# Expert weights in 16 KB runs, and the modulation's bias pieces in turns of their own

## The chip, the core and the metric

One Trainium2 chip; the kernel runs on one of its cores, in one launch. The metric is the device time in microseconds. Shorter is better.

## What is computed

Two transformer blocks one after the other, in float32. There are 256 tokens of width 1024 (16 learned ones go before them in the first block). The first block has two kinds of attention side by side, a gated join, and a SwiGLU layer. The second modulates its input with a vector made from `c`, runs retention and dilated attention, joins them, and ends in a mixture of 32 experts of which each token takes 4:

```python
def second_block(x, c, w_ada, ...):
    cs = jax.nn.silu(c)
    mod = cs @ w_ada[l] + b_ada[l]                  # 6 x 1024 values
    sh_a, sc_a, gt_a, sh_f, sc_f, gt_f = jnp.split(mod, 6, axis=-1)
    h = modulate(rms_norm(x, g_mix[l]), sh_a, sc_a)
    ret, att = retention(...), dilated_attention(...)
    merged = sigmoid(ga) * (ret @ w_ret_o) + sigmoid(gb) * (att @ w_att_o)
    x = x + gt_a * (merged @ w_o)
    h = modulate(rms_norm(x, g_ffn[l]), sh_f, sc_f)
    x = x + gt_f * moe(h, ...)
    return rms_norm(x, g_final)

def expert_block(xb, e):                            # in moe, for each of 32 experts
    u = xb @ w1[e] + b1[e]                          # 1024 x 2048, 8 MB
    glu, lin = clipped u[:, ::2], clipped u[:, 1::2]
    return (glu * sigmoid(1.702 * glu) * (lin + 1)) @ w2[e] + b2[e]   # 1024 x 1024, 4 MB
```

## The kernel before, in words

The program is written out as straight code in two stages.

**Dense stage.** All matrix products but the experts' are "w" and "t_" operations in a list, `plan`. Each takes a weight tile of 1 MB (128 partitions x 2048 values) that `feed_loads` (line 137) loads through the SyncE (SP) queue into a ring of two. `feed_halves` (155) splits a half of a tile into a high and a low part: ScalarE copies the high part (line 106) and VectorE subtracts (107). Three halves of split operands (`SPL`) can stand ready. TensorE multiplies them in three products (lines 213 to 215) in `run_w`: 12 matmuls for each of two column groups of a half, and after each 12 a call of `tick` (176). `tick` moves the side work on: attention heads, norms, and `ada`, each a generator that yields the number of ticks that it wants to rest. So the place of side work in the engines' order is set by ticks, when the program is built. When heads are closed (`close_heads`, 558), ticks run without matmuls between them.

**Modulation and biases.** `ada` (251) makes the 48 columns of `mod`: a row of 128 x 1024 values is loaded by `row` (265) through the GpSimd (POOL) queue, and one VectorE instruction (line 280) multiplies it by `cs` and sums it. From row 18 on (`LAG["bp"]`), each turn begins with a piece of `bias_parts` (987): a load of expert biases (994), six GpSimd instructions that split them into three bfloat16 parts (995 to 1000), and a store (1001). There are six pieces. Rows and pieces share one pool tag, `wa`, with two buffers. While `st["hold"]` is set (around the last down products of the first block), `ada` rests. The order of a turn is

```python
            if j >= LAG["bp"]:
                next(more, 0)
            if j < 47:
                rows.append(row(j + 1))
            yield LAG["ada"]
```

**Expert stage.** 384 weight tiles of 1 MB come in a fixed sequence: for each expert 8 of w_mlp1 (line 1055, 128 runs of 8 KB), then 4 of the expert before of w_mlp2 (1057, 256 runs of 4 KB); the last four (1064) in runs of 2 KB. Tiles of 8 KB per partition, "homes", take them in turn, 21 of them (`where`, line 1040): some are freed buffers of the dense stage (tags `b` and `c`), some are pools opened when parts of the dense stage close. `mload` (1043) issues loads through SP up to a number of tiles, `mst["room"]`, that grows from 5 to 13 while the dense stage runs; from then on a load is written behind each tile that TensorE has used, 21 tiles ahead. The first product is at line 1265 (8 matmuls per tile), the second at 1299. Per expert there are also transposes (1283), a weighted sum (1316) and, every second expert, a gather of tokens (1189). `last_tile` (1352) handles the last expert's second product.

**Buffers.** `big` has a tag `b` of 10 buffers with 8 KB per partition; a `pair` (high and low part) takes two.

Of the kernel before, what the change touches and what calls it, by code (L numbers as in the profile page):

```python
# [20 lines left out]
P = 128  # L21
D = 1024
S = 256
# [13 lines left out]

LAG = dict(rs=2, ad0=1, lam=4, bq=12, el=4, bp=18, r1=52, wo=3, rg=21, ada=7, head=6, ffn=2, n2=3, n2b=6, sb0=4, sb1=6, vt=3, df0=1, df1=4, df2=3, df3=8, df4=4, rt0=6, rt1=6, dl0=2, dl1=4, dl2=11, dl3=1)
LAG["in"] = 4
# [3 lines left out]
def tile_two_blocks(ctx, tc, A, out, dbg=None):  # L43
# [26 lines left out]
    def bigt(name, n=S, dt=F32, k=KT, wide=False):  # L70
        if n > S or wide:
            return big.tile([P, k, n], dt, tag="c", name=name, bufs=3)
        return big.tile([P, k, n], dt, tag="b", name=name, bufs=10)

    def pair(name, n=S, wide=False):
        return bigt(name + "h", n, F32R, wide=wide), bigt(name + "l", n, F32R, wide=wide)

    def flat(name):
        return big.tile([P, 2048], F32, tag="b", name=name, bufs=10)

# [10 lines left out]
    nr = flat("nr")  # L91
    sqa, sqb, sqg, rs0, rr = nr[:, 0:512], nr[:, 512:1024], nr[:, 1024:1536], nr[:, 1536:1792], nr[:, 1792:2048]
    ones, tri, ident = (cst.tile([P, P], F32, tag="c_" + n, name=n) for n in ("ones", "tri", "ident"))
# [157 lines left out]
    def ada():  # L251
# [30 lines left out]


# [44 lines left out]
    def norm_in():  # L328
        h, l = pair("xn", L)
        st["xn"] = (h, l)  # L330
        a = tmp.tile([P, 2, L], F32, tag="wa", name="sqa", bufs=2)
        b = flat("sqt")[:, 0:6 * L].rearrange("p (k i n) -> p k i n", k=3, i=2)
        for k in range(0, KT, 2):
# [180 lines left out]
    def branch(name, mov, key, nk=8):  # L514

        def first(c):
            def f(ps):
                if c == 0:
                    st[key] = bigt(key)
# [144 lines left out]
    def norm2(sq):  # L664
# [13 lines left out]
        st["r2"] = r2.unsqueeze(1).to_broadcast([P, 2, S])  # L678
        f = bigt("f2")
        for k in (0, 4):  # L680
# [42 lines left out]
    for c in range(4):  # L723
        def rgs(ps, c=c):
            if c == 0:
                st["rg"] = bigt("rg")
            while "r2" not in st:
                tick()
            if c == 0:
                st["shw"] = tmp.tile([P, KT], F32, tag="shw", name="shw", bufs=1)  # L730
# [67 lines left out]
    def dil_pair(jp):  # L798
# [18 lines left out]
        def bias():  # L817
            if jp == 0:
                at = bigt("at", S, F32R)
                st["at"] = at[:, 0:4, :], at[:, 4:8, :]  # L820
# [63 lines left out]
    def open_ret():  # L884
        nonlocal hd
        close_heads(dil_head)
        pools["mra"] = ctx.enter_context(tc.tile_pool(name="mra", bufs=3, side="right", reuse_waits="tile"))
        hd = heads.enter_context(tc.tile_pool(name="hd3", bufs=2, side="right", reuse_waits="tile"))
        mst["room"] = 8
        st["dec"] = hd.tile([P, 4, S], F32, tag="dec", name="dec", bufs=1)  # L890
# [3 lines left out]
    def close_ret():  # L894
        close_heads(ret_head)
        pools["mrb"] = ctx.enter_context(tc.tile_pool(name="mrb", bufs=2, side="right", reuse_waits="tile"))
        mst["room"] = 10

# [11 lines left out]


    branch("w_att_o_2", lambda: st["at"], "yat", 4)
    for c in range(4):
# [58 lines left out]
    def moe_consts():  # L972
        q = nc.scalar
        m = cst.tile([P, 1024], F32, tag="m", name="m")
        st["gtf"], st["iota"], st["spare"] = m[:, 0:512], m[:, 768:992], m[:, 992:1024]
# [11 lines left out]
    def bias_parts():  # L987

        nc.gpsimd.dma_start(sel, A["sel"])
        for c in range(6):  # L990
# [10 lines left out]
            nc.gpsimd.dma_start(bsd.ap()[:, c_], r)  # L1001
            yield

# [35 lines left out]
    pools, own = {}, {}  # L1039
    where = ["b"] * 5 + ["mra"] * 3 + ["mrb"] * 2 + ["b"] * 3 + ["mrc"] * 2 + ["mrd"] * 3 + ["c"] + ["mre"] * 2 + ["c"]  # L1040
    R = len(where)

    def mload(upto):
        while mst["load"] <= min(upto, mst["room"] - 1):
            i = mst["load"]
            kind, e, k = seq[i]
            j = i % R
            if where[j] in "bc":
                if j not in own:
                    own[j] = big.tile([P, 2048], F32, tag=where[j], name="mw", bufs=10 if where[j] == "b" else 3)  # L1050
                t = own[j]
            else:
                t = pools[where[j]].tile([P, 2048], F32, tag="mw", name="mw")
            if kind == 1:
                nc.sync.dma_start(t, A["w_mlp1_2"][e, k * P:(k + 1) * P, :])
            elif e < NE - 1:
                nc.sync.dma_start(t.rearrange("p (k n) -> p k n", k=2),
                                  A["w_mlp2_2"][e, k * 2 * P:(k + 1) * 2 * P, :].rearrange("(k p) n -> p k n", p=P))
            else:

                src = A["w_mlp2_2"][e, k % 2 * 512:(k % 2 + 1) * 512, k // 2 * 512:(k // 2 + 1) * 512]
                for kk in range(0, 4, 4 if k < 3 else 2):
                    n = 4 if k < 3 else 2
                    nc.sync.dma_start(t.rearrange("p (k n) -> p k n", k=4)[:, kk:kk + n], src.rearrange("(k p) n -> p k n", p=P)[:, kk:kk + n])
            wt[kind, e, k] = t
            mst["load"] += 1

# [12 lines left out]
    for o in plan:  # L1080
# [4 lines left out]
        if key == ("w_ffn_gate", LAG["el"]):  # L1085
            mst["room"] = 5
        if key == ("w_in_2", 12):
# [4 lines left out]
        if o is plan[-1]:  # L1092
            break
        mst["room"] = {("w_in_2", 33): 12, ("w_ret_o_2", 3): 13}.get(key, mst["room"])
        for _ in range(3 if state["load"] == len(wops) else 1):
            if mst["load"] < mst["room"]:
                mload(mst["load"])
    mload(mst["room"] - 1)
# [52 lines left out]
    mm(rpv[:, 1, :], tris, mask[:, 1, :], start=False, stop=True)  # L1151
    ht = flat("ht").rearrange("p (t d) -> p t d", t=2)
    xps += [residual(c) for c in range(2, 4)]
# [39 lines left out]

    xeb = flat("xe")
    xe = [xeb[:, b * 1024:(b + 1) * 1024].rearrange("p (k n) -> p k n", k=KT) for b in range(2)]
# [6 lines left out]

    pools["mrc"] = ctx.enter_context(tc.tile_pool(name="mrc", bufs=2, reuse_waits="tile"))
    pools["mrd"] = ctx.enter_context(tc.tile_pool(name="mrd", bufs=3, reuse_waits="tile"))
    mt = ctx.enter_context(tc.tile_pool(name="mt", bufs=2, reuse_waits="tile"))
    pools["mre"] = ctx.enter_context(tc.tile_pool(name="mre", bufs=2, reuse_waits="tile"))
    pu = ctx.enter_context(tc.tile_pool(name="pu", bufs=2, space=PSUM, reuse_waits="tile"))
# [223 lines left out]
    with tc.If(items > 0):  # L1431
        with tc.For_i(0, items, 1) as it:
# [20 lines left out]
            for k in range(KT):  # L1453
                z = lw[3 + k % 3]
                nc.sync.dma_start(z, A["w_mlp1_2"][bass.ds(ex, 1), k * P:(k + 1) * P, :].rearrange("o p n -> p (o n)"))
                up_k(u, xx[:, k, :], lambda hf, c: z[:, hf * 1024 + c * 512:hf * 1024 + (c + 1) * 512], k)
# [4 lines left out]
            for k2 in range(4):  # L1461
                z = lw[3 + (k2 + 2) % 3]
                nc.sync.dma_start(z.rearrange("p (k n) -> p k n", k=2),
                                  A["w_mlp2_2"][bass.ds(ex, 1), k2 * 2 * P:(k2 + 1) * 2 * P, :].rearrange("o (k p) n -> p (o k) n", p=P))
                for kk in range(2):
# [98 lines left out]
def layout(inp):  # L1564
# [39 lines left out]
```

## Time and profile before

| | us |
|---|---|
| median of three runs | 1827.83 |
| lowest and highest | 1824.49, 1828.0 |
| the profiled execution | 1826.24 |
| its span, first to last instruction | 1824.0 |
| TensorE, VectorE, ScalarE, GpSimd busy | 1739.4, 875.0, 484.7, 123.9 |

The span has 25,881 instructions; 571.82 MB are moved, 313 GB/s over the whole, in 107,645 packets. Mean granted TensorE clock 0.986. A matmul is counted busy from its start to its modelled end, and matmuls overlap, so a busy TensorE is not one at its peak; the number of matmuls in a stretch tells more. "Idle before" is the time in which an engine stood before an instruction, with what ended it. The lines named are those of the kernel before.

### The profile page before, as it was taken

How to read it: one execution, taken by the hardware profiler on the slowest of the kernel's cores; microseconds unless marked ns; L12 is line 12 of the kernel's file. 1: busy time of each engine (PE TensorE's matmuls, PEld its weight loads, DVE VectorE, ACT ScalarE, POOL GpSimd, SP SyncE). 2: the span in 40 equal slices, each digit the busy share in tenths (PEclk: the TensorE clock that was granted, in tenths of full speed). 3: DMA queues.
4: the chain of work that ended last, by engine and by line, in shares of the span. 5: the costliest groups of instructions: out<-in, count | busy, mean ns of one | idle time of the engine just before them, and what ended most of it. 6: DMA issues, size and time to landing. Idle time of an engine off the chain costs nothing. (4 is left out here: it accounts for less than half of the span.)

```text
span 1824.0 us, 25881 instructions
## 1 busy us (share of the span) xinstructions
PE 1739.4 (95%) x10942; PEld 1145.8 (63%) x10942; DVE 875.0 (48%) x1330; ACT 484.7 (27%) x754; POOL 123.9 (7%) x132
## 2 busy tenths in 40 slices
PE   8999998789999999999999999999999999999987
PEld 7999998789998999999733333333233323332322
DVE  7767776577778667776422223222222222222223
ACT  4545654244435644455300000000000000000001
POOL 2100004520003000000100000000000000000000
PEclk8999999799999999999999999999999999999999
DMA  6446455468665654566899999999999999999996
GB/s 220 170 167 229 158 193 186 167 209 341 245 216 179 245 179 168 204 223 226 309 416 424 423 425 424 424 422 424 422 425 424 423 424 423 424 423 425 422 425 261
DMA packets 107645, 571.82 MB, mean 313 GB/s; under 512 B 11022, under 2 KB 16070, under 8 KB 59654
## 3 DMA queue, kind: packets, MB, share of 16 engines
q1 hardware_dynamic: 96144, 538.46, 74.1%
q0 software_dynamic: 7904, 28.08, 4.6%
q10 hardware_dynamic: 3478, 3.59, 0.6%
q8 instruction: 87, 1.43, 0.3%
q14 instruction: 32, 0.26, 0.0%
HBM read 568.44 MB, written 4.02 MB: 314 GB/s over the span
## 5 line engine op out<-in xcount | busy, mean ns | idle before, releaser
L1265 PE MATMUL u<-mw,xe 128*64 128x512 f32 x2048 | 476.7, 600 | 18.1 <-DMA mw<-in_w_mlp_dram 17.3
L107 DVE TENSOR_TENSOR hl<-w,hl 128x1024 fp32r<-128x1024 f32 (+1 forms) x256 | 318.3, 1257 | 146.6 <-ACT hl L106 146.1
L1265 PEld LDWEIGHTS u<-mw,xe 128*64 128x64 f32 x2048 | 132.7, 136 | 300.1 <-issue 222.8
L106 ACT ACTIVATE hl<-w 128x1024 fp32r<-128x1024 f32 (+1 forms) x256 | 260.1, 1032 | 125.2 <-PE ps L215 74.7
L1299 PE MATMUL y<-mw,aT 128*64 128x512 f32 x992 | 227.7, 597 | 19.6 <-DMA mw<-in_w_mlp_dram 19.4
L1299 PEld LDWEIGHTS y<-mw,aT 128*64 128x64 f32 x992 | 67.2, 136 | 163.2 <-issue 102.0
L1319 DVE TENSOR_TENSOR macc<-macc,cp 128x512 f32<-128x512 f32 x124 | 79.7, 684 | 184.4 <-PE cp L1316 184.4
L213 PE MATMUL ps<-xnh,hl 128*128 128x256 f32 (+1 forms) x512 | 153.3, 299 | 2.4 <-ACT hl L106 2.4
L215 PE MATMUL ps<-xnh,hl 128*128 128x256 f32 (+1 forms) x512 | 149.2, 291 | 6.2 <-DVE hl L107 6.2
L214 PE MATMUL ps<-xnl,hl 128*128 128x256 f32 (+1 forms) x512 | 148.2, 289 | 0.0
L1285 ACT COPY aT<-ap 128x512 f32<-128x512 f32 x31 | 18.2, 586 | 425.6 <-PE ap L1283 425.6
L213 PE MATMUL ps<-h2h,hl 128*128 128x256 f32 x384 | 110.2, 287 | 0.0
L215 PE MATMUL ps<-h2h,hl 128*128 128x256 f32 x384 | 108.7, 283 | 0.0
L214 PE MATMUL ps<-h2l,hl 128*128 128x256 f32 x384 | 108.6, 283 | 0.0
L213 PEld LDWEIGHTS ps<-xnh,hl 128*128 128x128 f32 x512 | 99.2, 194 | 7.3 <-ACT hl L106 3.8
L215 PEld LDWEIGHTS ps<-xnh,hl 128*128 128x128 f32 x512 | 99.0, 193 | 7.3 <-DVE hl L107 7.3
L213 PE MATMUL ps<-hnh,hl 128*128 128x256 f32 x352 | 100.6, 286 | 0.0
L214 PE MATMUL ps<-hnl,hl 128*128 128x256 f32 x352 | 100.3, 285 | 0.0
L215 PE MATMUL ps<-hnh,hl 128*128 128x256 f32 x352 | 100.2, 285 | 0.0
L214 PEld LDWEIGHTS ps<-xnl,hl 128*128 128x128 f32 x512 | 99.0, 193 | 0.1
L1305 DVE TENSOR_TENSOR ys<-y,m 128x512 f32<-128x512 f32 x31 | 21.4, 692 | 138.4 <-PE y L1303 138.4
L1293 DVE COPY m<-gq 128x256 f32<-128x256 f32 x31 | 13.2, 425 | 144.1 <-PE gq L1291 144.1
(466 smaller groups left out, 2934.6 us busy)
## 6 DMA issues: line engine op xcount, KB each, us to landing
mw<-in_w_mlp_dram SPq DMA_DIRECT2D x383, 1024.0 KB, 19.7
w<-in_w_in_dram SPq DMA_DIRECT2D x60, 1024.0 KB, 4.9
wa<-in_w_ada_dram POOLq DMA_DIRECT2D x48, 512.0 KB, 4.8
w<-in_w_ffn_gate_dram SPq DMA_DIRECT2D x11, 1024.0 KB, 5.0
w<-in_w_ffn_up_dram SPq DMA_DIRECT2D x11, 1024.0 KB, 4.8
w<-in_w_gate_dram SPq DMA_DIRECT2D x8, 1024.0 KB, 5.4
w<-in_w_ffn_down_dram SPq DMA_DIRECT2D x8, 1024.0 KB, 5.4
w<-in_w_br_sb_dram SPq DMA_DIRECT2D x4, 1024.0 KB, 6.0
```

The lines of the kernel that those rows point to most:

```text
L106: act(hi, src, AF.Copy)
L107: (eng or nc.vector).tensor_sub(lo, src, hi.bitcast(F32))
L213: mm(ps[m], hi[:, k, cs], xh[:, k0 + k, r], start=first, stop=False, skip_group_check=True)
L214: mm(ps[m], hi[:, k, cs], xl[:, k0 + k, r], start=False, stop=False, skip_group_check=True)
L215: mm(ps[m], lo[:, k, cs], xh[:, k0 + k, r], start=False, stop=last, skip_group_check=True)
L1265: mm(u[64 * hf:64 * hf + 64, c * 512:(c + 1) * 512], xk, wcol(hf, c), start=k == 0, stop=False)
L1285: nc.scalar.copy(aT, ap)
L1293: nc.vector.tensor_copy(gT, gq[:, :256])
L1299: mm(y[64 * hf:64 * hf + 64, :], a, wcol(hf), start=k == 0, stop=False)
L1305: nc.vector.tensor_mul(ys, y, gtf)
L1319: nc.vector.tensor_add(d, d, cp[hf])
```

## The change

It does two things.

*The modulation.* `ada` loads two rows before it begins and then, in each turn, reduces a row first, then does a piece of the biases if one is due and rests `LAG["bq"]` = 12 ticks after it, and only then loads the row after next. The rest in a turn is 6 ticks, not 7.

*The experts' weights.* w_mlp1 and w_mlp2 are laid out in DRAM so that two tiles of a partition lie side by side, 16 KB; w_mlp2 of the last expert is laid out once more in the order in which it is read, in runs of 8 KB. Homes have 16 KB: 11 of them, nine that take a pair in one load of 2 MB and two that are made of two parts of 8 KB and take single tiles. To make room in such units, `big`'s tag `b` has 5 buffers of 16 KB; a pair of high and low parts is one buffer, and some arrays now share one: masks with the norms' sums (`mn`), and later users of the same halves (`f2`, `rg`, `yat`).

```diff
-LAG = dict(..., ada=7, ...)
+LAG = dict(..., ada=6, ...)
...
+    def double(name, dt=F32):
+        t = big.tile([P, 2, 2048], dt, tag="b", name=name, bufs=5)
+        return t[:, 0], t[:, 1]
...
-    mk = flat("masks")
+    mk, nr = double("mn")
...
-        rows = [row(0)]
+        rows = [row(0), row(1)]
         for j in range(48):
-            if j >= LAG["bp"]:
-                next(more, 0)
-            if j < 47:
-                rows.append(row(j + 1))
             yield LAG["ada"]
             while st.get("hold"):
                 yield 2
             t = rows.pop(0)
             nc.vector.tensor_tensor_reduce(out=t, in0=t, in1=cs, ...)
+            if j >= LAG["bp"] and next(more, 1) is None:
+                yield LAG["bq"]
+            if j < 46:
+                rows.append(row(j + 2))
...
-    where = ["b"] * 5 + ["mra"] * 3 + ["mrb"] * 2 + ["b"] * 3 + ["mrc"] * 2 + ["mrd"] * 3 + ["c"] + ["mre"] * 2 + ["c"]
-    R = len(where)
+    homes = ["b"] * 2 + ["mra", "mrb"] + ["b"] * 2 + [("mrs", "mrt"), "mrc", "mrd", ("c", "c"), "mre"]
+    R = 2 * len(homes)
...
+            home = homes[j // 2]
+            n = 1 if isinstance(home, tuple) else 2
+            if n == 2 and i + 1 > min(upto, mst["room"] - 1):
+                break
...
-                nc.sync.dma_start(t, A["w_mlp1_2"][e, k * P:(k + 1) * P, :])
+                src = A["w_mlp1_2"] if kind == 1 else A["w_mlp2_2"]
+                nc.sync.dma_start(t, src[e, k // 2, :, k % 2 * 2048:(k % 2 + n) * 2048])
...
-            mst["room"] = 5
+            mst["room"] = 4
...
-        mst["room"] = {("w_in_2", 33): 12, ("w_ret_o_2", 3): 13}.get(key, mst["room"])
+        mst["room"] = {("w_in_2", 33): 10, ("w_ret_o_2", 3): 13}.get(key, mst["room"])
```

The orders of TensorE and ScalarE stay as they are. VectorE's instructions are the same, with the modulation's reductions (the two "ISA" rows of line 280, now 283) at other places. The first place is the end of the gates and the first two output groups of w_out. `L107` (now 114) is the split of a half, `L529` a gate, `L547` to `L549` a join (now 538, 556 to 558), `L581` the residual of w_out (now 590). Before:

```order
L529 TENSOR_TENSOR gt<-ps,masks 128x512
L107 TENSOR_TENSOR hl<-w,hl 128x1024 x2
L280 ISA wa,mod<-wa,cs,c_vecs 128x1024
L280 ISA mod 128x1
L547 TENSOR_TENSOR gt<-gt,ysb 128x512
L548 TENSOR_TENSOR gt<-gt,ps 128x512
L549 TENSOR_TENSOR gt<-gt 128x512
L107 TENSOR_TENSOR m1l<-gt,m1h 128x512
L107 TENSOR_TENSOR hl<-w,hl 128x1024 x2
L581 TENSOR_TENSOR xr<-ps,xr 128x2x256
```

And now:

```order
L283 ISA wa,mod<-wa,cs,c_vecs 128x1024
L283 ISA mod 128x1
L538 TENSOR_TENSOR gt<-ps,mn 128x512
L114 TENSOR_TENSOR hl<-w,hl 128x1024 x2
L556 TENSOR_TENSOR gt<-gt,sy 128x512
L557 TENSOR_TENSOR gt<-gt,ps 128x512
L558 TENSOR_TENSOR gt<-gt 128x512
L114 TENSOR_TENSOR m_2817<-gt,m_2817 128x512
L114 TENSOR_TENSOR hl<-w,hl 128x1024 x2
L590 TENSOR_TENSOR xr<-ps,xr 128x2x256
```

The reduction that stood right ahead of the last join stands two splits and a gate earlier, and the one before it has gone from this stretch.

On GpSimd the pieces and rows keep their order (piece, then a row, six times); after the last piece 13 rows, not 19, come before the norm's products, and ten, not five, behind them.

The second place is SP's queue at the end of the dense stage, where the loads of w_o (line 145, now 152) and of the experts (1055 and 1057, now 1078) alternate. Before:

```order
L145 DMA w<-in_w_o_dram 128x2048 x2
L1055 DMA mw<-in_w_mlp_2_dram 128x2048
L145 DMA w<-in_w_o_dram 128x2048
L1055 DMA mw<-in_w_mlp_2_dram 128x2048
L145 DMA w<-in_w_o_dram 128x2048
L1055 DMA mw<-in_w_mlp_2_dram 128x2048 x4
L1057 DMA mw<-in_w_mlp_2_dram 128x2x1024 x4
```

And now:

```order
L152 DMA w<-in_w_o_dram 128x2048 x2
L1078 DMA mw<-in_w_mlp_2_dram 128x4096
L152 DMA w<-in_w_o_dram 128x2048
L1078 DMA mw<-in_w_mlp_2_dram 128x4096
L152 DMA w<-in_w_o_dram 128x2048
L1078 DMA mw<-in_w_mlp_2_dram 128x2048 x2
L1078 DMA mw<-in_w_mlp_2_dram 128x4096 x2
```

The loads between those of w_o have 2 MB each, and further on pairs and singles follow each other.

## Rows read from the trace of the kernel before

**Rows 1.** The page: DMA busy tenths and GB/s in 40 equal slices.

```profile
DMA  6446455468665654566899999999999999999996
GB/s 220 170 167 229 158 193 186 167 209 341 245 216 179 245 179 168 204 223 226 309 416 424 423 425 424 424 422 424 422 425 424 423 424 423 424 423 425 422 425 261
```

**Rows 2.** Windows: busy us (x instructions) per engine, granted clock, DMA share, GB/s.

```profile
270.00:290.00 20.00, 20.00 (x171) 20.00 (x170) 17.25 (x18) 9.30 (x12) 9.11 (x8) 1.00 0.67 250
290.00:390.00 100.00, 75.37 (x535) 73.20 (x534) 62.65 (x70) 37.91 (x51) 46.37 (x48) 0.85 0.49 173
390.00:410.00 20.00, 20.00 (x169) 20.00 (x168) 14.98 (x19) 8.64 (x11) 1.06 (x2) 1.00 0.70 230
```

**Rows 3.** Waits from 285 to 375 us: total us, times, longest.

```profile
DVE wa L280 <- DMA wa<-in_w_ada_dram: 25.5, 5, 10.1
ACT m1h L106 <- DVE gt L549: 24.9, 2, 16.2
...
PE ps L213 <- ACT m1h L106: 10.4, 1, 10.4
...
PE ss L320 <- DVE nr L316: 6.0, 1, 6.0
```

**Rows 4.** Timeline of VectorE, 284 to 375 us: start, us, instruction, idle before.

```profile
298.01 1.29 DVE L280 CUSTOM_DVE_ANT_0 wa<-wa,cs,c_vecs 128x1024 f32<-128x1024 f32 x1 [5.64 <-DMA wa<-in_w_ada_dram]
...
331.76 1.28 DVE L280 CUSTOM_DVE_ANT_0 wa<-wa,cs,c_vecs 128x1024 f32<-128x1024 f32 x1 [10.13 <-DMA wa<-in_w_ada_dram]
...
364.96 1.28 DVE L280 CUSTOM_DVE_ANT_0 wa<-wa,cs,c_vecs 128x1024 f32<-128x1024 f32 x1 [3.23 <-DMA wa<-in_w_ada_dram]
```

**Rows 5.** Timeline of GpSimd, same columns: a store and rows of the modulation.

```profile
290.78 0.58 POOL L267 DMA_DIRECT2D wa<-in_w_ada_dram  x1 [2.27 <-DMA bias_parts<-b]
...
324.30 0.52 POOL L1001 DMA_DIRECT2D bias_parts<-b  x1 [0.30 <-POOL b L1000]
327.18 0.58 POOL L267 DMA_DIRECT2D wa<-in_w_ada_dram  x1 [2.36 <-DMA bias_parts<-b]
...
375.36 1.12 POOL L267 DMA_DIRECT2D wa<-in_w_ada_dram  x2 [2.02 <-DMA bias_parts<-b]
```

**Rows 6.** Windows of the expert stage, columns as in rows 2.

```profile
1000.00:1100.00 100.00, 100.00 (x492) 36.93 (x492) 28.30 (x50) 5.91 (x10) 0.00 (x0) 1.00 1.02 424
...
1300.00:1400.00 100.00, 92.99 (x445) 32.55 (x442) 24.91 (x46) 4.72 (x8) 0.00 (x0) 1.00 1.02 423
```

**Rows 7.** Windows of the second block, columns as in rows 2.

```profile
700.00:800.00 100.00, 100.00 (x801) 98.60 (x800) 74.27 (x122) 43.39 (x63) 1.55 (x1) 1.00 0.54 188
840.00:880.00 40.00, 40.00 (x338) 39.92 (x337) 24.33 (x28) 18.93 (x25) 4.75 (x4) 1.00 0.68 256
```

**Rows 8.** DMA from 951 to 959, 962 to 970 and 920 to 1790 us.

```profile
DMA packets 867, 3.35 MB, mean 419 GB/s; under 512 B 54, under 2 KB 54, under 8 KB 861
...
q1 hardware_dynamic: 867, 3.35, 102.1%
...
DMA packets 461, 3.38 MB, mean 423 GB/s; under 512 B 49, under 2 KB 49, under 8 KB 49
...
q1 hardware_dynamic: 460, 3.37, 100.0%
...
q1 hardware_dynamic: 65657, 367.80, 101.4%
q8 instruction: 31, 0.51, 0.2%
```

**Rows 9.** Timeline of TensorE, 896 to 912 us: second to fifth tile.

```profile
902.95 1.94 PE L1265 MATMUL u<-mw,xe 128*64 128x512 f32 x8
...
906.80 5.37 PE L1265 MATMUL u<-mw,xe 128*64 128x512 f32 x24
```

**Rows 10.** The page: DMA issues, KB each, median us to landing.

```profile
mw<-in_w_mlp_dram SPq DMA_DIRECT2D x383, 1024.0 KB, 19.7
```

**Rows 11.** Timeline of SP's queue, 840 to 960 us.

```profile
862.81 0.33 SPq L145 DMA_DIRECT2D w<-in_w_o_dram  x1
```

More of the change, by code (lines that the diff above doesn't have):

```diff
@@ L72, in bigt, with rows8 @@
             return big.tile([P, k, n], dt, tag="c", name=name, bufs=3)
[L73 removed]
+        raise ValueError(name)
+    def double(name, dt=F32):
+        t = big.tile([P, 2, 2048], dt, tag="b", name=name, bufs=5)
+        return t[:, 0], t[:, 1]
+    def rows8(t):
+        return t.rearrange("p (k n) -> p k n", k=KT)
     def pair(name, n=S, wide=False):
[L76 to L79 removed]
+        if n > S or wide:
+            return bigt(name + "h", n, F32R, wide=wide), bigt(name + "l", n, F32R, wide=wide)
+        return [rows8(t) for t in double(name, F32R)]
     xr = bigt("xr", L)
@@ L886, in open_ret @@
         close_heads(dil_head)
-        pools["mra"] = ctx.enter_context(tc.tile_pool(name="mra", bufs=3, side="right", reuse_waits="tile"))
+        pools["mrs"] = ctx.enter_context(tc.tile_pool(name="mrs", bufs=1, side="right", reuse_waits="tile"))
+        pools["mra"] = ctx.enter_context(tc.tile_pool(name="mra", bufs=1, side="right", reuse_waits="tile"))
         hd = heads.enter_context(tc.tile_pool(name="hd3", bufs=2, side="right", reuse_waits="tile"))
-        mst["room"] = 8
+        mst["room"] = 6
         st["dec"] = hd.tile([P, 4, S], F32, tag="dec", name="dec", bufs=1)
@@ L895, in close_ret @@
         close_heads(ret_head)
-        pools["mrb"] = ctx.enter_context(tc.tile_pool(name="mrb", bufs=2, side="right", reuse_waits="tile"))
-        mst["room"] = 10
+        pools["mrb"] = ctx.enter_context(tc.tile_pool(name="mrb", bufs=1, side="right", reuse_waits="tile"))
+        mst["room"] = 8
     rd = [{}, {}]
@@ L973, in moe_consts @@
         q = nc.scalar
-        m = cst.tile([P, 1024], F32, tag="m", name="m")
+        m = cm
         st["gtf"], st["iota"], st["spare"] = m[:, 0:512], m[:, 768:992], m[:, 992:1024]
@@ L1047, in mload @@
             j = i % R
-            if where[j] in "bc":
+            home = homes[j // 2]
+            n = 1 if isinstance(home, tuple) else 2
+            if n == 2 and i + 1 > min(upto, mst["room"] - 1):
+                break
+            home = home if n == 2 else home[j % 2]
+            if home in "bc":
                 if j not in own:
-                    own[j] = big.tile([P, 2048], F32, tag=where[j], name="mw", bufs=10 if where[j] == "b" else 3)
+                    own[j] = big.tile([P, n * 2048], F32, tag=home, name="mw", bufs=5 if home == "b" else 3)
                 t = own[j]
             else:
-                t = pools[where[j]].tile([P, 2048], F32, tag="mw", name="mw")
-            if kind == 1:
-                nc.sync.dma_start(t, A["w_mlp1_2"][e, k * P:(k + 1) * P, :])
-            elif e < NE - 1:
-                nc.sync.dma_start(t.rearrange("p (k n) -> p k n", k=2),
-                                  A["w_mlp2_2"][e, k * 2 * P:(k + 1) * 2 * P, :].rearrange("(k p) n -> p k n", p=P))
-            else:
[L1061 to L1066, printed above, removed]
+                t = pools[home].tile([P, n * 2048], F32, tag="mw", name="mw")
+            if kind == 2 and e == NE - 1:
+                for m in range(n):
+                    for z in range(0, 2048, 2048 if k + m < 3 else 1024):
+                        w_ = 2048 if k + m < 3 else 1024
+                        nc.sync.dma_start(t[:, m * 2048 + z:m * 2048 + z + w_], A["w_mlp2_last"][k + m, :, z:z + w_])
+            else:
+                src = A["w_mlp1_2"] if kind == 1 else A["w_mlp2_2"]
+                nc.sync.dma_start(t, src[e, k // 2, :, k % 2 * 2048:(k % 2 + n) * 2048])
+            for m in range(n):
+                wt[kind, e, k + m] = t[:, m * 2048:(m + 1) * 2048]
+            mst["load"] += n
     def take(*key):
```

44 lines of the change are left out of this document (23 added, 21 removed).

## The prediction

> **What bounds the kernel now.** I read the page's slices first, then tables of stretches, then the waits. The span has two halves. Until about 890 us the dense work runs and TensorE is the bound: in the second block it is busy all the time (100.00 of 100 us, 40.00 of 40 [rows 7]), while the DMA engines are about half busy. From about 910 us the experts run, and there every slice of DMA is full, at 422 to 425 GB/s [rows 1]. Two places in this are not at their bound's pace.
>
> The first is 290 to 390 us. The 20 us on either side of it issue 171 and 169 matmuls; the 100 us between them issue 535 where 850 fit, and their granted clock is 0.85, so part of them ran at 1.2 GHz, the lower of the two levels [rows 2]. 315 missing matmuls at 20 us / 170 = 0.118 us are 37 us. The waits of this stretch say why: VectorE sat 25.5 us, in five waits, until a row of the modulation landed, and behind it ScalarE waited 24.9 us for the gate products, and TensorE 10.4 us for the joined operand that comes of them and 6.0 us for the norm's sum [rows 3]. The first of the five took 5.64 us, the longest 10.13, the last 3.23 [rows 4]. GpSimd shows their origin. It issues a row only after a whole piece of the biases: with the store of the piece at 324.30 us it still waits 2.36 us for that store, issues the row at 327.18, and the row comes to VectorE at 331.76 [rows 4, 5]. From the first row behind a piece to the last there are five turns, (375.36 - 290.78) / 5 = 16.9 us each [rows 5]. VectorE asks faster: `tick` runs after every 12 matmuls, 12 x 0.118 = 1.4 us, and a row is due every 7 ticks, 9.9 us. VectorE is in order, so all splits behind the row wait too.
>
> The second is the expert stage. TensorE issues 492 matmuls per 100 us early in it and 445 later [rows 6]. So at first it works off the experts loaded ahead, at its own pace, and then it runs at the pace of the transfers, some 10% slower. What ends the kernel is the queue of weights, full since about 915 us.
>
> **The change, part by part.**
>
> *Biases in turns of their own.* After a piece the side work now rests 12 ticks, then comes the row, then 6 ticks: 18 ticks, 25.6 us, per piece, against GpSimd's 16.9 us; and a row is used two such turns after the piece that it stood behind. So the five waits go. What stays of the 37 us: the norm's sum, 6.0 - 3.23 = 2.8 us; about 1 us at each of the four output groups of w_out, where VectorE has the residual and two splits to do; some 4 us at the lower clock after these pauses. That is 11, so I take **-26 us**. Ends: -13, if half of the waits was hidden behind operands already split, and -33. A pause in TensorE is not handed down to anything that could absorb it: the experts start when the dense work ends, and their stream starts with them.
>
> *Rows every 6 ticks, not 7.* The 18 rows before the first piece come closer together, and ten rows instead of five now stand behind the hold. Five more rows of 1.28 us [rows 4] are some 6.5 us of VectorE in a stretch of over 100 us where it is 74% busy and TensorE is full [rows 7]: nothing, covered by VectorE's idle time; if that cover fails, up to 3 us.
>
> *Runs of 16 KB.* One load now moves 2 MB; per partition it reads one run of 16 KB where a w_mlp1 tile had 8 KB and a w_mlp2 tile two of 4 KB. Nine homes in eleven take pairs; two are split in two singles, so 18 tiles of 22 come in pairs. The trace has no load with 16 KB packets, so I work from the two that it has. In a stretch of w_mlp2 alone, 807 packets of 4 KB and 6 of 8 KB took 102.1% of 16 engines for 8 us, 130.7 us, so 159.7 ns each; in one of w_mlp1, 411 of 8 KB took 128.0 us, 311.4 ns each [rows 8]. Twice the first less the second is a fixed 8.0 ns per packet. The records overlap: 101.4% over 870 us and 65,657 packets [rows 8] is 0.014 x 870 x 16 / 65,657 = 3.0 ns each, so 5.0 ns net. In the 356 tiles from the first steady ones to the last expert's w_mlp2, each of the 16 engines is spared 4 packets for each of 236 w_mlp1 tiles and 12 for each of 120 w_mlp2 tiles, by 18/22, and 8 for the 22 single w_mlp2 tiles: 772 + 1178 + 175 = 2125. At 5.0 ns this is **-11 us**. Ends: 0, if the fixed part is wholly hidden under the next packet, and 8.0 ns, -17 us. The Trainium skill ("DMA: Bandwidth & Descriptors", section "Why small descriptors are slow (HBM only)") gives a fixed overhead of about 3 cycles per packet and calls joining packets worth it at 256 bytes and less only; at the 850 MHz that the page gives for the fabric I estimate from it 3.5 ns, 7.5 us here, and the sum would be 3.5 us less of a gain. The rows show more than that.
>
> *Homes of 16 KB.* A home now comes free when TensorE is done with both its tiles, and both can be read only when both have landed. At the start the first reused home waits for the second tile: that one begins at 902.95 us, the third at 906.80 [rows 9], so the load goes out one tile, 3.9 us, later; but there are 22 tiles of room for 21. Together about 0. Later 8 loads are on their way (19.7 us to landing [rows 10] at some 2.47 us each); 8 pairs leave 3 homes to TensorE, which works on one or two. At the end the last pair of the 31st expert's w_mlp2 lands together, so one tile more is worked off behind it, 5.37 / 3 = 1.8 us [rows 9], less what the last expert's own tiles save in 8 KB runs instead of 2 KB: **+1 us**.
>
> *SP's queue.* Two 2 MB loads now stand between the last loads of w_o. Each is 2.5 us longer. The w_o load issued at 862.81 [rows 11] would land some 5 us later, and TensorE runs full from 840 to 880 us on operands split ahead [rows 7], so I cost it at nothing; without that cover twice 2.5 us. Of sharing one home between two arrays (masks and norm sums; the later uses as f2, rg, yat) I expect no wait: each new user comes a stage after the last reader.
>
> Sum: the profiled execution's 1826.24 us (span 1824.0) - 26 - 11 + 1 = 1790.2. The median of the runs is 1.6 us above that execution, so **1792**.
>
> **The rivals.**
>
> *Bytes, not packets, set the stream.* The fixed part is then hidden, and only the dense stage gains: 1827.8 - 26 + 1 = 1803. For it: w_mlp1 and w_mlp2 stretches differ little, 423 and 419 GB/s [rows 8]. Against: they differ. The Trainium skill's same page, section "Measured (HBM→SBUF, 128 partitions, SWDGE, issued from GpSimd)", has 425 GB/s for 16 MB, which would leave the 423 of this stage almost nothing; the trace agrees with that level for 8 KB runs and can't show it for longer ones. Chance 0.17.
>
> *Half of the waits returns elsewhere.* VectorE is the most loaded helper of the dense stage, and the pause may come back as waits for splits around w_out: -13 - 11 + 1, 1805. Chance 0.15.
>
> *More on both.* All 8 ns and the -33: 1779. Chance 0.12.
>
> *The rows wait as before.* GpSimd's queue still holds piece, store, row in that order; if 18 ticks shrink, as when heads are drained with ticks that hold no matmul, the waits stay: about 1816. Speaks against it: the row due next is already there, loaded before the piece. Chance 0.04.
>
> *Longer packets cost more, and it ends slower.* The one row with 16 KB packets is the fetch of instructions: 31 of 0.51 MB take 0.2% of 870 us x 16 [rows 8], about 0.9 us each, where 612 ns is what my fit gives net. The 146 pairs are 1168 packets per engine. At 621 ns the stage gains nothing; from 643 ns it eats the dense gain too; at 660 it costs 45 us and the kernel takes 1848. Against it: these fetches go elsewhere than SBUF, and from 4 to 8 KB the price per byte falls. Chance 0.08, of which 0.03 lie near no change.
>
> **How the numbers follow.** The forecast has the remaining 0.44. Its own range, from the ends of the two terms, is about 1780 to 1800. The first two rivals end at 1803 and 1805, so a range from 1776 to 1808 takes them in with the larger gain; 1816 and the slower case are left out, with the edges some 2 in 10. 0.2% is 3.7 us, about what a measurement of this kernel can tell from no change. All cases but the last are faster by more: 0.92; the last gives 0.03 for the same and 0.05 for slower.
>
> **What would show it.** Right: no wait of VectorE for a row from 240 to 480 us; some 760 matmuls or more in the 100 us that held 535 (the same part of the work begins earlier by then); the experts starting some 26 us earlier; 428 to 430 GB/s in the later slices, with about half the packets; 2 MB loads landing after 30 to 40 us (8 of 4.9 us) with no gap in the DMA row. Wrong: matmuls still missing around w_out with ScalarE's splits or the norm named; fewer than 424 GB/s; DMA slices under 9 in the expert stage.

## The result and the profile after

The changed kernel takes 1793.99 us (median of 4 runs, 1793.94 to 1794.62), the kernel before 1827.91 us beside it: a ratio of 0.9826, 95% interval 0.9813 to 0.9839. Forecast was 1792, between 1776 and 1808. The profiled execution has 1793.98 us and a span of 1791.8, against 1824.0: 32.2 us less.

The page after, DMA busy tenths and GB/s in 40 slices; from it also the issues of the experts' loads (number, KB each, median us to landing):

```profile
DMA  6556556568656654566899999999999999999995
GB/s 224 175 181 218 186 172 207 191 226 310 244 201 223 223 206 151 200 233 258 351 429 428 431 428 432 430 428 430 431 428 432 428 430 428 432 428 430 430 428 224
...
mw<-in_w_mlp_dram SPq DMA_DIRECT2D x156, 2048.0 KB, 31.5
mw<-in_w_mlp_dram SPq DMA_DIRECT2D x68, 1024.0 KB, 31.2
```

Where 422 to 425 GB/s stood [rows 1] there are now 428 to 432, with no gap, and a load of 2 MB lands after 31.5 us (before: 1 MB after 19.7 [rows 10]). The windows around the gates and w_out after, columns as in rows 2:

```profile
270.00:290.00 20.00, 20.00 (x156) 20.00 (x157) 13.65 (x16) 8.63 (x12) 1.11 (x2) 0.91 0.56 190
290.00:390.00 100.00, 97.26 (x803) 96.35 (x802) 74.62 (x85) 51.77 (x67) 32.98 (x35) 1.00 0.60 210
390.00:410.00 20.00, 20.00 (x169) 20.00 (x168) 16.03 (x17) 7.70 (x9) 8.37 (x8) 1.00 0.77 303
```

The 100 us that held 535 matmuls hold 803, at a full clock. But the 20 us ahead, 171 matmuls in rows 2, hold 156 at 0.91: something was lost there. The waits from 285 to 375 us after:

```profile
POOL b L1004 <- DVE mod L283: 55.2, 4, 16.4
DVE hl L114 <- ACT hl L113: 12.6, 16, 2.1
...
PE ss L328 <- DVE mn L324: 1.4, 1, 1.4
```

VectorE's 25.5 us for rows [rows 3] are gone. The wait has changed sides: GpSimd, for which no other engine waits in these rows, now waits for VectorE. GpSimd's timeline after, two rows of the modulation two turns apart:

```profile
301.05 0.58 POOL L274 DMA_DIRECT2D wa<-in_w_ada_dram  x1 [1.71 <-DMA bias_parts<-b]
...
353.54 0.58 POOL L274 DMA_DIRECT2D wa<-in_w_ada_dram  x1 [1.86 <-DMA bias_parts<-b]
```

(353.54 - 301.05) / 2 = 26.2 us per turn (25.6 forecast), where GpSimd alone set 16.9 [rows 5]. The first tile of the experts on TensorE (count, ns min/median/max, first and last start), before and then after:

```profile
L1265 PE MATMUL u<-mw,xe x16: 592/592/644, 899.1 to 904.3; 128*64 128x512 f32 x16
```

```profile
L1280 PE MATMUL u<-mw,hx x114: 590/592/644, 873.9 to 904.9; 128*64 128x512 f32 x114
```

25.2 us earlier. The transfers from 920 to 1700 us, before and then after:

```profile
DMA packets 58882, 330.23 MB, mean 423 GB/s; under 512 B 5031, under 2 KB 5031, under 8 KB 32172
```

```profile
DMA packets 27184, 335.11 MB, mean 430 GB/s; under 512 B 3016, under 2 KB 3016, under 8 KB 3016
```

Fewer than half the packets, 4.88 MB more.

**The balance.** Two rulers serve for all that follows. TensorE issues the same 10,942 matmuls in the same order in every kernel, so the start of its n-th can be compared; and a tile has landed when the last of its DMA packets ends. Numbering the experts' tiles from 0: the first tile's use is 25.2 us earlier (899.10 to 873.88); from there to the landing of tile 23 it takes 15.87 us, not 12.24 (+3.6); from that to the landing of tile 367, 841.18, not 854.40 (-13.2); from that to the use of tile 368, 8.36, not 4.60 (+3.8); from that to the end 1.1 less. The sum is -32.2, the difference of the spans.

### The profile page after: what moved, and what is told of

The parts are those of the page before. It is cut to its first block, busy times and chain, and to the rows that moved or that the text cites. A ratio compares the mean times of both kernels' runs of the same rounds, so it can differ in the third digit from the quotient of the medians.

```text
span 1791.8 us, 25574 instructions
## 1 busy us (share of the span) xinstructions
PE 1722.1 (96%) x10942; PEld 1143.3 (64%) x10942; DVE 871.6 (49%) x1330; ACT 484.7 (27%) x754; POOL 120.0 (7%) x132
## 5 line engine op out<-in xcount | busy, mean ns | idle before, releaser
L1280 PE MATMUL u<-mw,hx 128*64 128x512 f32 x2048 | 472.8, 600 | 19.2 <-DMA mw<-in_w_mlp_dram 18.1
L1280 PEld LDWEIGHTS u<-mw,hx 128*64 128x64 f32 x2048 | 135.4, 136 | 293.8 <-issue 244.1
L1314 PEld LDWEIGHTS y<-mw,aT 128*64 128x64 f32 x992 | 72.0, 138 | 154.2 <-issue 126.8
L220 PE MATMUL ps<-h,hl 128*128 128x256 f32 x384 | 110.2, 287 | 0.0
L221 PE MATMUL ps<-h,hl 128*128 128x256 f32 x384 | 108.8, 283 | 1.2 <-DVE h L114 1.2
L222 PE MATMUL ps<-h,hl 128*128 128x256 f32 x384 | 108.6, 283 | 0.0
L1308 DVE COPY m<-gq 128x256 f32<-128x256 f32 x31 | 13.2, 425 | 140.5 <-PE gq L1306 140.5
## 6 DMA issues: line engine op xcount, KB each, us to landing
mw<-in_w_mlp_dram SPq DMA_DIRECT2D x156, 2048.0 KB, 31.5
```

The costliest lines, as they stand in the source:

```text
L220: mm(ps[m], hi[:, k, cs], xh[:, k0 + k, r], start=first, stop=False, skip_group_check=True)
L221: mm(ps[m], hi[:, k, cs], xl[:, k0 + k, r], start=False, stop=False, skip_group_check=True)
L222: mm(ps[m], lo[:, k, cs], xh[:, k0 + k, r], start=False, stop=last, skip_group_check=True)
L1280: mm(u[64 * hf:64 * hf + 64, c * 512:(c + 1) * 512], xk, wcol(hf, c), start=k == 0, stop=False)
L1308: nc.vector.tensor_copy(gT, gq[:, :256])
L1314: mm(y[64 * hf:64 * hf + 64, :], a, wcol(hf), start=k == 0, stop=False)
```

## The experiments

Medians of whole runs stand in the first table, each beside runs of the kernel before on the same chip; in the second the rulers, from the profiled executions. In it, "1600-2000" is how much later (+) or earlier (-) than in the kernel before TensorE got from its 1600th to its 2000th matmul, and so on.

| kernel | us, median | before | ratio, 95% interval |
|---|---|---|---|
| e1 turns alone | 1799.67 | 1825.69 | 0.9858 (0.9843 to 0.9873) |
| e2 runs and homes alone | 1821.0 | 1825.69 | 0.9974 (0.9963 to 0.9986) |
| e3 no rest | 1820.52 | 1825.69 | 0.9971 (0.9959 to 0.9982) |
| e4 rest, one row ahead, 7 ticks | 1789.71 | 1825.69 | 0.9805 (0.979 to 0.982) |
| e5 pairs as two loads | 1797.55 | 1826.59 | 0.9845 (0.9829 to 0.9862) |
| e6 before, w_mlp1 in 4 KB | 1837.35 | 1826.59 | 1.0062 (1.0046 to 1.0079) |
| e7 change, 7 ticks | 1787.76 | 1826.59 | 0.9792 (0.9775 to 0.9808) |
| e8 other order of homes | 1791.68 | 1826.59 | 0.9817 (0.98 to 0.9833) |
| e9 first loads later | 1795.72 | 1826.06 | 0.9837 (0.9822 to 0.9852) |
| e10 7 ticks, last pairs split | 1787.59 | 1826.06 | 0.9787 (0.9772 to 0.9803) |
| e11 all four | 1789.43 | 1826.06 | 0.9803 (0.979 to 0.9817) |
| e12 three of them | 1783.03 | 1826.28 | 0.9769 (0.9755 to 0.9783) |

| kernel | 1600-2000 | 2000-2600 | 3000-3200 | first tile at | landing 23 to 367 |
|---|---|---|---|---|---|
| before | | | | 899.10 | 854.4 |
| the change | +4.6 | -32.3 | +1.6 | 873.88 | 841.2 |
| e1 | +3.8 | -31.5 | 0.0 | 871.47 | 854.8 |
| e2 | 0.0 | 0.0 | +3.1 | 901.43 | 841.4 |
| e3 | +5.1 | -5.3 | +3.5 | 901.03 | 842.5 |
| e4 | 0.0 | -30.6 | +1.8 | 869.39 | 842.4 |
| e7 | 0.0 | -31.1 | +0.6 | 866.66 | 842.6 |
| e9 | +4.6 | -32.3 | 0.0 | 877.55 | 842.3 |

**The two parts apart.** My theory was that they act in separate stages and add up. e1 is the kernel before with the diff's lines in `ada` and `ada=6`, nothing else.

> The kernel before with the modulation's new turns alone (rows two ahead, 12 ticks of rest after a piece, 6 ticks otherwise); weights and homes as before. My theory, that the two parts add up and each acts in its own stage: the dense stage gives its 25 us (first tile of the experts on TensorE near 874 us, not 899), the expert stage runs as before at 422 to 425 GB/s, so about 1802 us, -25 us against the kernel before. Rival 1, the start of the experts is handed down only in part because the transfers end the kernel: less than -20 us. Rival 2, the earlier experts need the longer runs to be fed: the gain is under -10 us.

e2 is the changed kernel with the old lines of `ada` and `ada=7`.

> The changed kernel with the modulation's old turns (one row ahead, 7 ticks, no rest): runs and homes of 16 KB alone. My theory: the five waits of VectorE for rows are back, 25 us of them, the experts start near 899 us, and of the stream's -13 us some 7 us stay after the slower start and the pair at the end: about 1820 us, -7 to -8 us against the kernel before. Rival, only the bytes count and the shorter stream was due to the earlier start: 0, within 2 us of the kernel before.

e1 gained 26.0 us, e2 4.7, the change 33.9. Both rivals of e1 fall, and the rival of e2 by its stream: 841.4 us as in the change, at the old start. The gains of e1 and e2 add to 30.7, so the two parts add up but for 3.2 us. e2 missed its 7 to 8 us: it reaches the experts 2.3 us late, which the windows of e2 around w_out don't explain, as they repeat rows 2:

```profile
290.00:390.00 100.00, 74.01 (x534) 71.63 (x533) 62.37 (x69) 37.09 (x51) 45.78 (x48) 0.85 0.50 173
```

The loss is at 3000-3200, 3.1 us where the change loses 1.6, which is also a part of the 3.2; e9 below goes after it, and the rest of the 3.2 stays open.

**What took the waits away.** e3 takes the rest out of the changed kernel:

```diff
-            if j >= LAG["bp"] and next(more, 1) is None:
-                yield LAG["bq"]
+            if j >= LAG["bp"]:
+                next(more, 1)
```

> The changed kernel without the 12 ticks of rest after a piece of the biases; rows still two ahead. My theory, that the turn of VectorE must be longer than GpSimd's 16.9 us per piece and row: VectorE asks every 6 ticks, 8.5 us, the two rows of lead are used up after one or two turns, and VectorE waits again at three or four rows, 15 to 25 us in all; the kernel takes about 1814 us, +20 us against the changed kernel. Rival, the lead of two rows is what counts: no waits, within 3 us of the changed kernel.

e4 keeps the rest and takes the lead away, `ada=7` with it:

```diff
-        rows = [row(0), row(1)]
+        rows = [row(0)]
         for j in range(48):
+            if j >= LAG["bp"] and next(more, 1) is None:
+                yield LAG["bq"]
+            if j < 47:
+                rows.append(row(j + 1))
             yield LAG["ada"]
...
-            if j >= LAG["bp"] and next(more, 1) is None:
-                yield LAG["bq"]
-            if j < 46:
-                rows.append(row(j + 2))
```

> The changed kernel with rows one ahead again (piece first, then its row, as before; 7 ticks) but with the 12 ticks of rest after a piece, ahead of the row. My theory, that the rest counts and the lead does not: a row has 7 ticks, 9.9 us, to land after its issue and takes about 4.6 us, so no wait of VectorE for a row is left where TensorE is full, and the time is within 3 us of the changed kernel. Rival, the lead of two rows is needed: the waits come back in part, +8 us or more.

Without the rest the waits of VectorE return in spite of two rows of lead; the waits from 240 to 480 us of e3:

```profile
DVE wa L283 <- DMA wa<-in_w_ada_dram: 24.7, 7, 7.8
```

and TensorE gains 5.3 us in 2000-2600 instead of 32. With the rest and one row ahead there is no such wait, and 789 matmuls in the 100 us; e4's window:

```profile
290.00:390.00 100.00, 96.83 (x789) 96.23 (x789) 75.05 (x85) 50.69 (x67) 26.79 (x29) 0.98 0.59 204
```

So the rest did it: VectorE's turn must be longer than GpSimd's 16.9 us. No run tried a rest between none and 12 ticks. Rows two ahead only delay a shortage. e4 is at least as fast as the change, 36.0 us below the kernel before, not 33.9: it has not the +4.6 us at 1600-2000. With e7 below, which has two rows of lead, it agrees within the intervals (0.9805 and 0.9792).

**The pace of 6 ticks.** VectorE's timeline of the changed kernel, the three instructions of a join, and GpSimd's beside it:

```profile
263.58 1.46 DVE L556 TENSOR_TENSOR gt<-gt,sy 128x512 f32<-128x512 f32 x1 [0.81 <-ACT gt L555]
264.96 0.68 DVE L557 TENSOR_TENSOR gt<-gt,ps 128x512 f32<-128x512 f32 x1
265.67 1.03 DVE L558 TENSOR_TENSOR gt<-gt 128x512 f32<-128x512 f32 x1
```

```profile
263.32 1.16 POOL L1006 TENSOR_TENSOR b<-b 96x512 f32<-96x512 f32 x1
264.55 0.95 POOL L1007 CAST b<-b 32x512 bf16<-32x512 f32 x1
265.55 0.61 POOL L1008 CAST b<-b 32x512 bf16<-32x512 f32 x1
266.24 1.48 POOL L1009 TENSOR_TENSOR b<-b 32x512 f32<-32x512 f32 x1
```

A piece of the biases runs beside the join. And ahead of the join stands one more reduction of a row, which had to wait for its row first:

```profile
257.29 1.28 DVE L283 CUSTOM_DVE_ANT_0 wa<-wa,cs,c_vecs 128x1024 f32<-128x1024 f32 x1 [0.39 <-DMA wa<-in_w_ada_dram]
```

The windows right behind the join:

```profile
268.00:270.00 2.00, 0.64 (x3) 0.43 (x4) 1.87 (x3) 2.00 (x3) 1.26 (x2) 1.00 0.00 0
270.00:272.00 2.00, 2.00 (x11) 2.00 (x12) 2.00 (x3) 0.27 (x1) 0.14 (x1) 0.57 0.43 82
```

TensorE does 3 matmuls in 2 us, and then 11, where 17 fit, at a granted clock of 0.57, so mostly at 1.2 GHz, the lower of its two levels. Of the 4.6 us, 3.6 are lost here, between the 1920th and the 1942nd matmul. The other 1.0 is lost before the 1700th, where a reduction stands ahead of an instruction (line 468) for which TensorE waits 0.9 us. e7 changes only `ada=6` to `ada=7` in the changed kernel.

> The changed kernel with 7 ticks instead of 6 between the modulation's rows; two rows of lead and 12 ticks of rest stay. The trace of the changed kernel shows a loss of 3.6 us between its 1920th and 1940th matmul: a piece of the biases on GpSimd ran beside a join on VectorE, whose instructions took 1.46 and 1.03 us instead of 0.69, TensorE paused 2 us and ran 3.5 us at the lower clock. Theory, the pace of 6 ticks put the pieces there: at 7 ticks they come later, the loss is gone, and the experts start near 870 us instead of 874, 1788 to 1791 us in all. Rival, the order of row and piece decides, not the pace: first tile of the experts near 874 us, no change.

It takes 1787.76 us, 38.8 less than the kernel before, and the loss is 0.0, at both places. e7's join has no piece beside it, and the reduction comes behind the join, at 265.28 us:

```profile
260.21 0.69 DVE L556 TENSOR_TENSOR gt<-gt,sy 128x512 f32<-128x512 f32 x1 [0.95 <-ACT gt L555]
261.02 0.69 DVE L557 TENSOR_TENSOR gt<-gt,ps 128x512 f32<-128x512 f32 x1
261.74 0.69 DVE L558 TENSOR_TENSOR gt<-gt 128x512 f32<-128x512 f32 x1
```

Kernels with 6 ticks (the change, e1, e3, e5, e8, e9) lose 3.4 to 5.1 us at this place, those with 7 (e2, e4, e7, e10 to e12) nothing. So the pace is the cause: it brought the first piece, and a reduction, forward to a join. How much of the 3.6 us each of the two cost no run separates. From the timelines it is about as much VectorE time: from the last head's square on ScalarE (line 506) to the start of the join it takes 8.35 us in the change and 7.35 in e7, and the join's two long instructions are 1.1 us longer.

**The price of a packet.** e5 moves each pair of the changed kernel by two loads in runs of 8 KB:

```diff
-                nc.sync.dma_start(t, src[e, k // 2, :, k % 2 * 2048:(k % 2 + n) * 2048])
+                for m in range(n):
+                    c0 = (k % 2 + m) * 2048
+                    nc.sync.dma_start(t[:, m * 2048:(m + 1) * 2048], src[e, k // 2, :, c0:c0 + 2048])
```

> The changed kernel with each pair moved by two loads of 1 MB in runs of 8 KB instead of one of 2 MB in runs of 16 KB; homes, order and layout stay. Measured on the stretch from the landing of tile 23 to that of tile 367, which took 854.4 us before and 841.2 us with the change. Theory, a price per packet: about 1130 packets more per engine at 5 to 6.5 ns, so 847 to 848.5 us, and a rate of 426 to 427 GB/s; the pair's second tile is no longer tied to the first, which may give back 1 to 3 us at the start and the end of the stage. Rival, the gain came with the homes and the place of the weights in DRAM and not with the packets: 841 us as with the change. Rival, the number of loads counts as much as that of packets: nearer 854 us.

e6 cuts the runs of w_mlp1 in the kernel before in two, with the same loads and homes:

```diff
-                nc.sync.dma_start(t, A["w_mlp1_2"][e, k * P:(k + 1) * P, :])
+                nc.sync.dma_start(t.rearrange("p (h n) -> p h n", h=2), A["w_mlp1_2"][e, k].rearrange("h p n -> p h n"))
...
-    o["w_mlp1_2"] = a["w_mlp1_2"].reshape(32, D, 2 * D)
+    o["w_mlp1_2"] = np.ascontiguousarray(a["w_mlp1_2"].reshape(32, 8, P, 2, D).transpose(0, 1, 3, 2, 4))
```

> The kernel before with w_mlp1 laid out so that its loads of 1 MB come in runs of 4 KB instead of 8 KB; the same loads, homes and order. Theory, a price per packet: 1835 packets more per engine in the stretch from the landing of tile 23 to that of tile 367, at 5 to 6.5 ns, so 9 to 12 us: 863 to 866 us instead of 854.4, and a whole time of 1835 to 1838 us. Rival, only the bytes count between 4 and 16 KB: 854 us and no change of the whole.

The same 780 us (920 to 1700) of e5 and of e6:

```profile
DMA packets 45626, 332.53 MB, mean 426 GB/s; under 512 B 5065, under 2 KB 5065, under 8 KB 5065
```

```profile
DMA packets 84587, 326.49 MB, mean 419 GB/s; under 512 B 4974, under 2 KB 4974, under 8 KB 84551
```

All four rows fill 780 x 16 = 12,480 engine-us. If a MB costs a fixed time and a packet c on top, two kernels with M1, M2 MB and n1, n2 packets give c = 12,480 (M1 - M2) / (M1 n2 - M2 n1). Before and e6, with equal loads: 12,480 x 3.74 / 8.71 million = 5.4 ns. Before and the change: 5.7. The change and e5: 5.2. The rulers say the same: e5 847.7 us (847 to 848.5 expected), e6 865.2 (863 to 866), so 5.8 and 5.9 ns for each packet more, and e6's whole run is 10.8 us longer. "Only bytes count" falls in both directions, and so does a price per load: e6 has as many loads as the kernel before. (e5 has more loads than the change as well as more packets; as its price isn't above e6's, nothing is left for them.) In the records a packet of 16 KB took 612 ns (the mean of 16,708 of the change in these 780 us), not the 900 of the instruction fetches.

**The start of the stage and its end.** e8 changes the order of homes:

```diff
-    homes = ["b"] * 2 + ["mra", "mrb"] + ["b"] * 2 + [("mrs", "mrt"), "mrc", "mrd", ("c", "c"), "mre"]
+    homes = ["b"] * 2 + ["mra", "mrb"] + ["b"] * 2 + ["mrc", ("mrs", "mrt"), "mrd", "mre", ("c", "c")]
...
-        mst["room"] = {("w_in_2", 33): 10, ("w_ret_o_2", 3): 13}.get(key, mst["room"])
+        mst["room"] = {("w_in_2", 33): 10, ("w_ret_o_2", 3): 12}.get(key, mst["room"])
```

> The changed kernel with the homes in another order: the pair mrc ahead of the two single parts mrs and mrt, the two single parts of tag c last, and 12 tiles of room instead of 13 before the last dense operands. Theory, the 3.6 us that the start of the expert stage lost stem from the single home mrt, whose load waits until 855 us, and everything behind it in SP's queue with it: landing of tile 23 minus the first use of a tile falls from 15.9 us to about 12, 3 to 5 us less in all. Rival, the transfers are then late at another home: no change.

From the first use to the landing of tile 23 it takes 13.7 us; 12 was expected. A miss for the most part: kernels with the change's order have 14.5 to 15.9 (e7 and the change), those with the new one 13.7 to 14.1 (e8 and e12), so about 1 us of the 3.6 came back; nor is it the grain of 2 MB, since e5 has 14.7. The transfers pause in all of them; GB/s in 40 slices of 1 us, the kernel before from 865 us, the change from 840 us, e12 (which has e8's order) from 833 us:

```profile
GB/s 393 410 451 451 197 279 418 279 0 0 0 66 221 459 418 393 418 385 401 348 33 86 336 410 238 86 336 430 410 397 455 410 393 426 467 377 285 225 256 348
```

```profile
GB/s 344 426 401 418 418 98 8 0 0 0 0 16 0 0 0 16 221 360 451 475 426 426 442 426 410 459 410 410 410 418 426 361 360 467 385 393 385 399 322 281
```

```profile
GB/s 311 393 262 57 8 0 0 0 0 0 0 246 229 377 475 410 360 434 442 401 418 434 303 319 344 360 410 360 442 360 442 426 385 401 410 434 426 395 244 199
```

The pause is shorter in e12, some 8 us instead of the change's 10, but the kernel before stands only 3 us, and 2 more later. SP's queue shows the same: counted from the first use, tile 13 goes out 30.5 us ahead of it before (at 868.57 us), and 18.9 in the change (855.01); in e8 the next load, tile 12, goes out 23.5 ahead. So in both orders the larger homes come free later than the old ones; which of the arrays holds them, no run shows.

e9 goes after the loss at 3000-3200. In SP's queue of the changed kernel the first two pairs stand among the loads of w_ffn_down:

```profile
397.54 0.33 SPq L152 DMA_DIRECT2D w<-in_w_ffn_down_dram  x1
397.92 0.42 SPq L1078 DMA_DIRECT2D mw<-in_w_mlp_dram  x1
402.56 0.33 SPq L152 DMA_DIRECT2D w<-in_w_ffn_down_dram  x1
402.94 0.42 SPq L1078 DMA_DIRECT2D mw<-in_w_mlp_dram  x1
409.44 0.33 SPq L152 DMA_DIRECT2D w<-in_w_ffn_down_dram  x1
```

and e9 lets them go later:

```diff
-        if key == ("w_ffn_gate", LAG["el"]):
-            mst["room"] = 4
         if key == ("w_in_2", 12):
             moe_consts()
+            mst["room"] = 4
```

> The changed kernel with its first two loads of experts, 2 MB each, let go later: at the output groups of the second w_in, not among the loads of w_ffn_down. Between its 3000th and 3200th matmul the changed kernel loses 1.6 us against the kernel before, and the changed kernel with old turns 3.1 us; ScalarE waits there twice, 10.1 us in all, for a load of w_ffn_down that stands behind a load of 2 MB. Theory, that load of 2 MB is the cause: the loss is 0 to 0.3 us, ScalarE's waits for w_ffn_down fall under 4 us, and the whole time by 1.5 to 2 us, which the times of whole runs may not tell apart. Rival, the shared buffers of the new homes are the cause: the loss stays.

The waits of ScalarE from 400 to 460 us, of the kernel before, of the change and of e9:

```profile
ACT hl L106 <- DMA w<-in_w_ffn_down_dram: 3.2, 1, 3.2
```

```profile
ACT hl L113 <- DMA w<-in_w_ffn_down_dram: 10.1, 2, 5.6
```

```profile
ACT hl L113 <- DMA w<-in_w_ffn_down_dram: 2.7, 1, 2.7
```

At 3000-3200 nothing is lost any more, as the theory had it, and the shared buffers, which e9 keeps, are cleared. But the whole is not shorter: from its 4400th to its 4600th matmul e9 loses 4.9 us instead, since its 2 MB now stand ahead of loads of w_in. ScalarE's waits in e9 from 570 to 610 us:

```profile
ACT hl L113 <- DMA w<-in_w_in_dram: 11.6, 4, 6.1
```

e10 is e7 with the last pairs split:

```diff
-                nc.sync.dma_start(t, src[e, k // 2, :, k % 2 * 2048:(k % 2 + n) * 2048])
+                step = n * 2048 if i < 364 else 2048
+                for z in range(0, n * 2048, step):
+                    nc.sync.dma_start(t[:, z:z + step], src[e, k // 2, :, k % 2 * 2048 + z:k % 2 * 2048 + z + step])
```

> The changed kernel with 7 ticks between rows, and with the pairs from tile 364 on moved by two loads of 1 MB each. With pairs the last tiles are used 4.2 to 7.6 us after they land, with single tiles of 1 MB 3.0 to 4.3 us. Theory, the end of the stream is passed on at the grain of a load: the use of tile 379 comes 2 to 3 us earlier after its landing, and the whole time is 2 us less than with 7 ticks alone, 1785 to 1787 us. Rival, the last expert is bound by the engines and not by the landing: no change of the whole, 1787 to 1789 us.

Tile 379 is used 4.4 us after it lands, not 6.9: 2.5 us earlier, as expected. From the landing of tile 367 to the end e10 takes 59.2 us and e7 60.7, so 1.5 us of it reach the end. The medians, 1787.59 and 1787.76, don't show it: e10's profiled execution reached the experts at 870.28 us and e7's at 866.66, with the same code up to there. Executions scatter by such amounts ahead of the experts (before and e6, whose loads up to there differ only in the runs of the first tiles: 899.10 and 895.34), so a term of 2 us is read from a ruler inside its stage and not from whole runs. e11 and e12 put the corrections together, with e9's place and without it.

> The changed kernel with all four corrections: 7 ticks between rows, the first loads of experts later, the other order of homes with 12 tiles of room, and the last pairs as two loads of 1 MB. If the losses that were found in the traces add up: 1793 - 5 (pace) - 1 (first loads) - 1 (start of the stage) - 2 (end) = 1784 us, and a ratio of about 0.977 to the kernel before. If they overlap: 1787 us, as with 7 ticks alone.

> The changed kernel with 7 ticks between rows, the other order of homes with 12 tiles of room, and the last pairs as two loads of 1 MB; the first loads of experts stay where the change has them. If the gains that the traces showed one by one hold together: 1788 - 1 (start of the stage) - 2 (end) = 1785 us, ratio 0.977. If whole runs scatter by as much as these terms: 1787 to 1789 us, as with 7 ticks alone.

e11 is no gain over e7, and loses 5.3 us at the place of e9's loss. e12, without e9's place, takes 1783.03 us (1782.22 to 1787.9), 43.3 less than the kernel before and 9.3 more than the change saved: the lowest of all, though its interval still touches e7's.

## Why the prediction was right, step by step

The direction, the two places and the total hold; 1794 against 1792. The total hides four terms that were off and cancel in part.

- *Biases in turns of their own*, -26. The waits went, and 2000-2600 gained 32.3 us, since of the 37 missing us not 11 stayed but about 5: the output groups' pauses and the time at the lower clock that I had kept as independent were mostly the train of the waits for rows. The norm's sum waits 1.4 us, not 2.8. What I took for the second cause, rows two ahead, is none (e3, e4).
- *Rows every 6 ticks*, 0, up to 3. This step failed: 4.6 us. I had counted the added reductions where TensorE is full, behind the hold; the cost came ahead of it, from where the pace puts the reductions and GpSimd's first piece (e7).
- *SP's queue*, 0. The place was wrong. I looked at w_o, where nothing is late; the first pairs stand among the loads of w_ffn_down, and a load of 2 MB ahead of one of these cost 1.6 us (3.1 in e2). Those three give 32.3 - 4.6 - 1.6 = 26.1, and the experts started 25.2 us earlier, near the forecast for the wrong reason.
- *Runs of 16 KB*, -11. My 2125 packets are the 356 tiles up to the last expert; on the 344 of the ruler the same working is 2125 x 344 / 356 x 5.0 = 10.3 us, and it measured 13.2 (about 12 in e4 and e7). How the gain divides between this and the start is loose by more than 1 us, the two together are not: from the first use to the landing of tile 367 it takes 857.0 us in the change, 856.9 to 857.3 in e2, e3, e4, e7 and e9, and 866.6 before, 9.6 less. The net price of 5.0 ns was 5.2 to 5.7 by the windows, 5.8 to 6.4 by the ruler. The estimate of 3.5 ns, worked out from the overhead per packet alone in the Trainium skill ("DMA: Bandwidth & Descriptors", section "Why small descriptors are slow (HBM only)"), is too low here. The section's limit of 256 bytes is about joining short descriptors into one packet; here the runs themselves grew, and it paid from 4 KB to 16.
- *Homes of 16 KB*, start about 0, end +1. This step failed too. "22 tiles of room for 21" is wrong, and so are the 21 homes in the description of the kernel before: `where` has 22 entries, so both kernels have 22 tiles of room, and nothing stood against the 3.9 us of the later load. The start cost 3.6 us, but hardly by that load: e5, whose tile 22 goes out 2.0 us after the first use as before (5.8 in the change), still needs 14.7. The longer pause ahead of the first use is the likelier cause; e8's order gives about 1 us back, and the rest is not tested. The end cost 2.7 (3.8 - 1.1), since both halves of a pair come late, not one tile once: with single loads (e10) 1.5 us of it came back.

Of the rivals, "bytes, not packets" and "longer packets cost more" are excluded by e5 and e6; "more on both" needed 8 ns a packet; "half of the waits returns" by the 803 matmuls. "The rows wait as before" is what e3 makes of the change, 1820.5 us: it would have needed only the rest to be missing.

## What to carry to other kernels

Where one engine fetches for another in order, compare the two turns: if the producer's (16.9 us here) is longer than the consumer's, a deeper queue only postpones the wait, and a rest at the consumer ends it. A stream at its bound still pays per packet, 5 to 6 ns from 4 to 16 KB here, so count packets as well as bytes; but larger loads make every queue and every hand-over coarser, so look at each place where one stands ahead of another stage's load, and split the last ones. Compare kernels of the same instruction order by the start of the n-th instruction: it finds losses of 2 us that whole runs hide.

## What the runs showed of the hardware

VectorE's join took 1.46 and 1.03 us instead of 0.69 beside GpSimd's arithmetic, while its middle instruction, which has one operand in PSUM, stayed at 0.68. The Trainium skill ("SBUF — State Buffer", section "SBUF: two separate sides") states that a VectorE instruction with two SBUF inputs and a GpSimd instruction that reads SBUF lock each other out of a shared pair of ports; the three rows agree. So does e5, where GpSimd's arithmetic on the piece begins later against the join: the first instruction stays at 0.69 us, and the third takes 1.69 beside a subtraction of 1.16. In the change these 1.1 us and the reduction ahead of the join became 3.6 on TensorE, by a pause and the lower clock behind it. And the price per packet is nearly the same from 4 to 8 KB (5.4 ns) as from 8 to 16 (5.2): it does not vanish up to there.
